# Small tiled matmuls of a hybrid decoder layer gathered into bursts, and weights converted one piece further ahead

## The chip, the cores and the metric

One core of one Trainium2 chip. Times are device microseconds of that core; the figure compared is the median of several executions.

## The reference, cut to what matters

One inference step of a decoder layer for 256 prompt tokens and 64 sample tokens (8 sequences of 8), 320 columns in all, in float32:

```
p = x @ w_in                          # 2048 -> 5408
y_lru  = rg_lru(conv(p[:1024])) * gelu(p[1024:2048])          # 8 blocks of 128 channels
y_rwkv = rwkv7_mix(p[2048:])          # 16 heads of 64; per token, per head:
#   S = S * w_t - (S kk_t) (kk_t a_t)^T + v_t k_t^T ;  o_t = S r_t ; group norm, bonus, gate
x = LN(ALPHA * x + concat(y_lru, y_rwkv) @ w_out)
x = LN(ALPHA * x + cross_attention(x, mem_k, mem_v, 4 heads of 512, 256 memory tokens) @ xa_wo)
x = LN(ALPHA * x + relu(x @ mlp_w1)**2 @ mlp_w2)              # 2048 -> 8192 -> 2048
```

The keys and values of the memory (`mem @ xa_wk`, `mem @ xa_wv`) and all final states are outputs too.

## The kernel before, in words

**Linear layers.** A weight comes in pieces of 128x1024 (512 KB), loaded by SyncE's queue into `wraw`. ScalarE rounds a piece to `wh` (the high part), and VectorE or GpSimd subtracts it to give `wl` (the low part); activations `u` are held in the same two parts. Each product of a 128x128 weight block is three TensorE matmuls: high x high, high x low, low x high (`mm_piece`, line 380). A piece holds 8 blocks, so 24 matmuls. The trace names the first two `ps<-u,wh` and the third `ps<-u,wl`. `Stream` (line 252) runs ahead: `get` (line 295) loads three pieces ahead and casts two ahead; there are 4 `wraw`, 3 `wh` and 3 `wl` buffers. `poll` issues the subtraction once the cast is done in planned time; which engine takes it is decided by `tt` (line 326), which adds `pool_wait` (6 us in the mixer, 0 after) to GpSimd's price.

**The stages.** In the mixer the input projection makes 43 tiles of 128 output columns: three code tiles, then r, k, v, x, g for each of eight pairs of heads. The memory's key projection follows (16 tiles of 256 columns), then the value projection, the output projection, the query projection with cross attention, its output projection, and the MLP.

**The planner.** Python generators emit the mixer's work, and `Sched` (line 117) decides at build time in which order the instructions stand in each engine's queue, by its own clock and costs. A generator yields `PE` ahead of TensorE work. `tick` (line 199) is called ahead of each group of three linear matmuls and emits every waiting TensorE step whose inputs are ready by the clock (plus 0.3 us), up to 2 us of them. So small matmuls stand between linear ones as soon as they are ready. `drain` (line 218) emits tasks in order of time with no linear work between.

**A pair of heads** (`rwkv`, line 624) takes these steps: two products for decay and rate (`code,lw`); head sums (128x32 tiling); scores of four chunks of 64 tokens (`AR,BK`, 64x64) and of the sample tokens; transposes (`K,BK`, `K,t`); a loop over four chunks; then centring, head sums, the gate product (`sg,lg`). Each chunk has three steps: a right-hand side (`S,AR` and `UV,GM`), a product with the inverse (`R,XT`), and the last step, which updates the state and the output (`UV,BT`, then `AR,S`, then `GM,UV`; names are moving operand, then stationary one). A product of 64x64 uses a quarter of the array, one of 128x64 half, and several stand beside each other; a float32 matmul appears as two records. `invert` (line 828) inverts a triangular matrix on GpSimd, with DMA round trips, and four TensorE steps (32x32); `sample` (line 906) does the 64 sample tokens in steps of its own.

**What holds pairs apart.** Pair p's transposes wait until pair p-2 is finished. When tile v of pair i is done, `on_win` (line 1023) drains pair i-3 if it still runs, and after the key projection everything is drained. `tmp` (line 519) has 18 work tiles. PSUM has 8 banks, one for each `ax()` (line 339).

Of the kernel before, what the change touches and what calls it, by code (L numbers as in the profile page):

```python
# [88 lines left out]
for _name, _w in (("mu", 27), ("w0", 8), ("a0", 8), ("kk", 8), ("ka", 8), ("rk", 8), ("lnw", 8), ("lnb", 8),  # L89
                  ("cw0", 8), ("cw1", 8), ("cw2", 8), ("cw3", 8), ("cb", 8), ("ba", 8), ("bx", 8), ("lam", 8),  # L90
                  ("g1", 16), ("b1", 16), ("g2", 16), ("b2", 16), ("g3", 16), ("b3", 16),
                  ("h0", 64), ("sh", 216), ("cv", 192)):
    VEC[_name] = _n
    _n += _w
NVEC = _n
# [10 lines left out]
NTMP = 18  # L106
NPB = 3
MARGIN = 0.3
QUEUE = 1.2
# [7 lines left out]
class Sched:  # L117
# [5 lines left out]
    def __init__(self):  # L123
        self.clock = 0.0
        self.free = {"V": 0.0, "A": 0.0, "G": 0.0}
        self.tasks = []
        self.cur = None
        self.table = 0
        self.poll = lambda: None

    def account(self, e, op, a, k):
# [4 lines left out]
        if e == "T":  # L136
            m = a[1].shape[-1]
            if a[1].dtype == F32R:
# [35 lines left out]
    def add(self, gen, name=None, after=0.0, eng=None):  # L174
        self.tasks.append(Task(gen, name, self.clock + after, eng is None, eng))
# [23 lines left out]
    def tick(self, budget=2.0):  # L199
        c0 = self.clock  # L200
        self.poll()
        moved = True
# [24 lines left out]
class Task:  # L227
    def __init__(self, gen, name, t, pe=True, eng=None):
        self.gen, self.name, self.t, self.pe, self.eng = gen, name, t, pe, eng


PE = "PE"
# [19 lines left out]
class Stream:  # L252


    def __init__(self, nc, sch, A, tt, raw, hp, lp, srcs, ahead_load, ahead_conv):
# [3 lines left out]
        self.al, self.ac = ahead_load, ahead_conv  # L259
        self.n_load = self.n_conv = 0  # L260
# [4 lines left out]
    def poll(self, upto=None):  # L265

        while self.pend:
# [6 lines left out]
            self.sch.cur = cur  # L274

# [19 lines left out]
    def get(self, i):  # L295
        while self.n_load < min(len(self.srcs), i + 1 + self.al):
# [7 lines left out]
def body(ctx, tc, I, O):  # L304
# [12 lines left out]
    pool_wait = [6.0]  # L317
# [19 lines left out]
    drp = ctx.enter_context(tc.tile_pool(name="dr", bufs=1, space=DRAM))  # L337

    def ax():
        return psp.tile([128, 512], F32, name="ps")  # L340
# [13 lines left out]

    sh_out = cst.tile([128, 27, 9], F32, name="sh_out")
# [1305 lines left out]
```

## Time and profile before

| what | value |
| --- | --- |
| median of three runs (lowest to highest) | 2049.2 us (2038.58 to 2050.24) |
| the profiled execution: its own time, its span | 2050.63 us, 2048.5 us |
| TensorE busy, matmul records | 1999.3 us (98%), 15750 |
| VectorE, ScalarE, GpSimd busy | 1054.7, 890.8, 430.3 us |
| mean granted clock of TensorE | 0.989 |
| weight pieces of the input projection, issue to landing | 4.7 us, 86 pieces |

TensorE's matmuls are pipelined and their ends are modelled, so that a record is longer than its share of the stream; what a matmul costs is read from the distance between starts. A busy TensorE can therefore still lose time between starts. The trace puts all engine work on one line, L246 (the wrapper `Eng` that accounts for it); instructions are told apart by their tiles.

### The profile page before, as it was taken

How to read it: one execution, taken by the hardware profiler on the slowest of the kernel's cores; microseconds unless marked ns; L12 is line 12 of the kernel's file. 1: busy time of each engine (PE TensorE's matmuls, PEld its weight loads, DVE VectorE, ACT ScalarE, POOL GpSimd, SP SyncE). 2: the span in 40 equal slices, each digit the busy share in tenths (PEclk: the TensorE clock that was granted, in tenths of full speed). 3: DMA queues.
4: the chain of work that ended last, by engine and by line, in shares of the span. 5: the costliest groups of instructions: out<-in, count | busy, mean ns of one | idle time of the engine just before them, and what ended most of it. 6: DMA issues, size and time to landing. Idle time of an engine off the chain costs nothing.

```text
span 2048.5 us, 38116 instructions
## 1 busy us (share of the span) xinstructions
PE 1999.3 (98%) x15750; PEld 1887.1 (92%) x15750; DVE 1054.7 (51%) x1604; ACT 890.8 (43%) x1452; POOL 430.3 (21%) x689
## 2 busy tenths in 40 slices
PE   8999999999999999999999999999999999999996
PEld 8987888788898998888899999999999999999996
DVE  6666666667545446544476444443444434443444
ACT  5655555455335335544334533334333333334333
POOL 0223022222214245322053300000000000001133
PEclk9999999999999999999999999999999999999998
DMA  7343343335467774688643444444444444445442
GB/s 249 127 125 99 102 132 119 106 109 172 140 197 249 241 213 150 239 318 305 234 142 120 144 147 152 151 148 151 148 154 145 154 148 152 150 149 152 147 147 90
DMA packets 120701, 333.79 MB, mean 163 GB/s; under 512 B 33056, under 2 KB 42304, under 8 KB 120528
## 3 DMA queue, kind: packets, MB, share of 16 engines
q1 hardware_dynamic: 105392, 279.59, 43.3%
q0 software_dynamic: 15136, 51.77, 7.0%
q8 instruction: 123, 2.02, 0.4%
q14 instruction: 50, 0.41, 0.1%
HBM read 315.66 MB, written 15.65 MB: 162 GB/s over the span
## 4 chain that ended last, share of the span: by engine, by line
PE 90%; DVE 3%; POOL 3%; issue 1%; DMA 1%; ACT 1%; SPq 0%; POOLq 0%; ACTq 0%; DVEq 0%
PE ps L246 90%; DVE wl L246 1%; DVE t L246 1%; POOL wl L246 1%; DVE u L246 1%; POOL tt L246 1%; POOL u L246 0%; POOL Xp L246 0%; ACT wh L246 0%; POOL r L246 0%; DMA t<-in_x 0%; DMA Xn<-bx 0%; DMA kv<-in_cache_k 0%; ACT u L246 0%; DMA Mp<-bm 0%
## 5 line engine op out<-in xcount | busy, mean ns | idle before, releaser
L246 DVE TENSOR_TENSOR wl<-wraw,wh 128x1024 fp32r<-128x1024 f32 x490 | 616.0, 1259 | 579.5 <-ACT wh L246 578.8
L246 ACT CAST wh<-wraw 128x1024 fp32r<-128x1024 f32 x502 | 526.1, 1048 | 652.9 <-PE ps L246 607.7
L246 PE MATMUL ps<-u,wh 128*128 128x320 f32 (+1 forms) x3424 | 764.0, 313 | 7.5 <-ACT u L246 6.6
L246 PE MATMUL ps<-r,wh 128*128 128x320 f32 x3072 | 681.9, 311 | 2.1 <-ACT r L246 1.8
L246 PEld LDWEIGHTS ps<-u,wh 128*128 128x128 f32 x3424 | 566.5, 190 | 27.9 <-issue 7.7
L246 PE MATMUL ps<-u,wl 128*128 128x320 f32 (+1 forms) x1712 | 525.9, 307 | 9.9 <-DVE wl L246 9.7
L246 PEld LDWEIGHTS ps<-r,wh 128*128 128x128 f32 x3072 | 515.8, 189 | 10.4 <-issue 7.5
L246 PE MATMUL ps<-r,wl 128*128 128x320 f32 x1536 | 476.5, 310 | 4.7 <-POOL wl L246 2.5
L246 PEld LDWEIGHTS ps<-u,wl 128*128 128x128 f32 x1712 | 324.8, 190 | 12.4 <-DVE wl L246 12.4
L246 PEld LDWEIGHTS ps<-r,wl 128*128 128x128 f32 x1536 | 289.8, 189 | 5.2 <-POOL wl L246 2.8
L246 PE MATMUL ps<-h,wh 128*128 128x320 f32 x1024 | 225.6, 309 | 0.0
L246 POOL TENSOR_TENSOR r<-r 128x320 f32<-128x320 f32 x64 | 46.0, 720 | 724.6 <-ACT r L246 724.6
L246 PEld LDWEIGHTS ps<-h,wh 128*128 128x128 f32 x1024 | 171.4, 188 | 0.2
L246 PE MATMUL ps<-h,wl 128*128 128x320 f32 x512 | 158.2, 309 | 0.0
L246 DVE TENSOR_TENSOR u<-u,ps 128x320 f32<-128x320 f32 x134 | 61.7, 484 | 78.2 <-PE ps L246 75.5
L246 ACT ACTIVATE r<-ps 128x320 f32<-128x320 f32 x64 | 28.0, 437 | 157.8 <-PE ps L246 157.8
L246 PEld LDWEIGHTS ps<-h,wl 128*128 128x128 f32 x512 | 96.1, 188 | 0.0
L246 POOL TENSOR_TENSOR tt<-Mp,Xp 40x15 f32<-40x15 f32 (+7 forms) x120 | 46.8, 390 | 191.8 <-DMA Mp<-bm 183.5
L246 POOL TENSOR_TENSOR s<-s,u 128x320 f32<-128x320 f32 x42 | 65.3, 1554 | 92.5 <-DVE u L246 92.3
L246 PE MATMUL ps<-wh,u 128*128 128x512 f32 x256 | 79.9, 391 | 0.0
L246 ACT ACT_TABLE_LOAD x48 | 61.6, 1283 | 9.2 <-DVE mxs L246 7.7
L246 PEld LDWEIGHTS ps<-wh,u 128*128 128x128 f32 x256 | 48.1, 188 | 10.1
(239 smaller groups left out, 1574.6 us busy)
## 6 DMA issues: line engine op xcount, KB each, us to landing
wraw<-in_w SPq DMA_DIRECT2D x256, 512.0 KB, 3.5
wraw<-in_w_in SPq DMA_DIRECT2D x86, 512.0 KB, 4.7
wraw<-in_wk SPq DMA_DIRECT2D x32, 512.0 KB, 4.7
wraw<-in_wv SPq DMA_DIRECT2D x32, 512.0 KB, 4.8
wraw<-in_w_out SPq DMA_DIRECT2D x32, 512.0 KB, 4.1
kv<-in_cache_k POOLq DMA_DIRECT2D x32, 512.0 KB, 6.6
wraw<-in_wq SPq DMA_DIRECT2D x32, 512.0 KB, 5.1
kv<-in_cache_v POOLq DMA_DIRECT2D x32, 512.0 KB, 8.7
```

Source lines behind the costliest of these rows:

```text
L246: r = f(*a, **k)
```

## The change

`Sched` knows the tiling of each TensorE step (`Mode`, rows x columns, with the number of PSUM banks it needs) and adds 0.093 us to its clock where the tiling changes. `tick` emits 128x128 steps at once, others only if 2.2 us have passed since the last of them or at least four are ready; then it prefers the tiling that the array has. Steps that need more banks than are free by the planner's count wait (`room`: 8, and 7 from tile 37 on).

In `rwkv` the scores of chunks and sample become one step of four banks, and the two groups of transposes one of three; the state product of the output (`AR,S`) moves from the last step of a chunk to the step of `R,XT`; the product `bv` moves ahead. In `sample` the identity product joins the right-hand side, and the last two steps become one, with its masked operand always made by VectorE. The decay products and head sums now wait for a burst. `attend_sample` yields the 128x32 tiling for its products.

`Stream` casts three pieces ahead, with 3 `wraw`, 4 `wh` and 4 `wl` buffers; it issues a load when the subtraction three pieces before is issued. `pool_wait` is 50 us in the mixer and 2 us after it. Work tiles fall from 18 of 356 columns to 16 of 348; the shift state is loaded into one of them, and three output tiles live only in the mixer.

```diff
-NTMP = 18
+NTMP = 16
 NPB = 3
 MARGIN = 0.3
+TURN = 0.093
+GAP = 2.2
+FULL = (128, 128)
...
+            mode = tuple(32 if x <= 32 else 64 if x <= 64 else 128 for x in (a[1].shape[0], m))
+            if mode != self.mode:
+                self.clock += TURN
+                self.mode = mode
...
-            task.pe = x == PE
+            task.pe = isinstance(x, Mode)
+            if task.pe:
+                task.mode, task.need = x.mode, x.need
...
-    def tick(self, budget=2.0):
-        c0 = self.clock
+    def tick(self):
         self.poll()
+        self.others()
+        ready, c0 = self.ready(), self.clock
+        tiled = c0 >= self.burst + GAP or sum(t.mode != FULL for t in ready) >= 4
+        while self.clock - c0 <= 3.0:
+            ready = [t for t in ready if tiled or t.mode == FULL]
+            if not ready:
+                break
+            self.step(next((t for t in ready if t.mode == self.mode), ready[0]))
+            if self.mode != FULL:
+                self.burst = self.clock
+            self.others()
+            ready = self.ready()
...
+    def ready(self):
+        return [t for t in self.tasks if t.pe and t.t + MARGIN <= self.clock and self.fits(t)]
+    def fits(self, task):
+        return not task.pe or self.room is None or self.live + task.need <= self.room
...
             for task in list(self.tasks):
-                if task not in self.tasks:
+                if task not in self.tasks or task.pe:
                     continue
-                if task.pe:
-                    ok = task.t + MARGIN <= self.clock and self.clock - c0 <= budget
-                else:
-                    ok = task.t <= self.clock + 0.1
-                    if task.eng:
-                        ok = ok and self.free[task.eng] <= self.clock + QUEUE
-                if ok:
+                if task.t <= self.clock + 0.1 and (not task.eng or self.free[task.eng] <= self.clock + QUEUE):
                     self.step(task)
                     moved = True
...
-            t = min(self.tasks, key=lambda t: t.t)
+            t = min([t for t in self.tasks if self.fits(t)], key=lambda t: t.t)
...
+PE, PE_HH, PE_FH, PE_FQ, PE_QQ, PE_HF = (Mode(*x) for x in ((128, 128), (64, 64), (128, 64), (128, 32), (32, 32), (64, 128)))
...
             cur, self.sch.cur = self.sch.cur, None
             self.tt(l, t, h.bitcast(F32), ALU.subtract)
             self.sch.cur = cur
+            self.n_low += 1
+            if self.n_load < len(self.srcs) and self.n_load < self.n_low + 3:
+                self.load()
...
     def get(self, i):
-        while self.n_load < min(len(self.srcs), i + 1 + self.al):
+        while self.n_load < min(len(self.srcs), self.n_low + 3):
             self.load()
         while self.n_conv < min(self.n_load, i + 1 + min(i, self.ac)):
...
-    pool_wait = [6.0]
+    pool_wait = [50.0]
...
-    rawp = ctx.enter_context(tc.tile_pool(name="wraw", bufs=4))
-    hp = ctx.enter_context(tc.tile_pool(name="wh", bufs=3))
-    lp = ctx.enter_context(tc.tile_pool(name="wl", bufs=3))
+    rawp = ctx.enter_context(tc.tile_pool(name="wraw", bufs=3))
+    hp = ctx.enter_context(tc.tile_pool(name="wh", bufs=4))
+    lp = ctx.enter_context(tc.tile_pool(name="wl", bufs=4))
...
+            yield PE_HF(2)
             pw, pa = ax(), ax()
             T.matmul(pw[:, :NTOK], lw[0:64, :], code[0:64, :], start=True, stop=True)
...
+            yield PE_HH(4)
             pg = [ax(), ax()]
             for c in range(4):
                 for s in range(2):
                     for i, h in enumerate(HS):
                         o, a = slots(i)[s]
                         mm(pg[i][o, c * 128:c * 128 + 128], BK[h, c, a, :], AR[h, c, :, :])
-            yield
-            for i in range(2):
-                V.tensor_mul(GM[:, i, 0:4], pg[i].rearrange("p (c a t) -> p c a t", c=4, a=2),
-                             MU[:, 0:1].to_broadcast([128, 4, 2, 64]))
-            sch.cur.t -= 1.0
-            yield PE
-            B4 = pp.tile([128, 2, 64], F32, name="B4")
-            UV4 = pp.tile([128, 2, 64], F32, name="UV4")
...
-            pt = [ax(), ax()]
+            yield PE_HH(3)
+            pt, pv = [ax(), ax()], ax()
             for c in range(4):
                 for s in range(2):
                     for i, h in enumerate(HS):
                         o, a = slots(i)[s]
                         mm(pt[i][o, c * 64:c * 64 + 64], BK[h, c, a, :], ident[h, h])
-            yield
-            for i in range(2):
-                copy(BT[:, :, 64 * i:64 * i + 64], pt[i][:, :256].rearrange("p (c x) -> p c x", c=4))
-            yield PE
-            pv = ax()
             for c in range(4):
                 for h in HS:
                     mm(pv[h, c * 64:c * 64 + 64], zv[h, c * 64:c * 64 + 64], ident[h, h])
             yield
+            for i in range(2):
+                copy(BT[:, :, 64 * i:64 * i + 64], pt[i][:, :256].rearrange("p (c x) -> p c x", c=4))
             for i, h in enumerate(HS):
...
+                yield PE_HH
                 for o in HS:
                     mm(pr[o, 64:128], XT[o, c, :], R[o, :])
+                if c:
+                    for h in HS:
+                        mm(po[h, c * 64:c * 64 + 64], S[h, :], AR[h, c, 1, :], True, False)
                 for i, o in enumerate(HS[::-1]):
                     copy(UV[o, c, i, :], pr[o, 64:128])
-                yield PE
+                yield PE_FH
                 for i, h in enumerate(HS):
                     mm(pr[h, 128:192], BT[:, c, 64 * i:64 * i + 64], UV[:, c, i, :])
                 Sn = p2.tile([128, 64], F32, name="S")
                     V.scalar_tensor_tensor(Sn, pr[:, 128:192], PT[:, c:c + 1], ts_, op0=mult, op1=add)
                 else:
                     V.tensor_scalar(Sn, pr[:, 128:192], PT[:, 0:1], None, op0=mult)
-                if c:
-                    for h in HS:
-                        mm(po[h, c * 64:c * 64 + 64], S[h, :], AR[h, c, 1, :], True, False)
+                free()
                 for i, h in enumerate(HS):
                     mm(po[h, c * 64:c * 64 + 64], UV[:, c, i, :], GM[:, i, c, 1, :], not c, True)
                 S = Sn
-                yield PE
+                if c < 3:
+                    yield PE_HH
+            yield
             nc.gpsimd.dma_start(O["Sp"][p], S)
...
-            yield PE
-            pr = ax()
+            free()
+            yield PE_HH(2)
+            pr, po = ax(), ax()
             for i, h in enumerate(HS):
                 mm(pr[HS[1 - i], 0:64], RO[h, 0, :], ident[h, h], True, False)
             for i, h in enumerate(HS):
                 mm(pr[HS[1 - i], 0:64], GM[h, i, 4, 0, :], UV[h, i, :], False, True)
             R = p1.tile([128, 64], F32, name="R4")
             copy(R, pr[:, 0:64])
-            yield PE
+            for h in HS:
+                mm(po[h, 0:64], ident[h, h], RO[h, 1, :], True, False)
+            yield PE_HH
             for o in HS:
                 mm(pr[o, 64:128], XT[o, 4, :], R[o, :])
             for i, o in enumerate(HS[::-1]):
                 copy(UV[o, i], pr[o, 64:128])
+            free()
             yield
             um = [p1.tile([128, 8, 64], F32, name=f"um{i}") for i in range(2)]
             for i in range(2):
-                tt(um[i], UV[:, i:i + 1, :].to_broadcast([128, 8, 64]),
-                                BM.unsqueeze(2).to_broadcast([128, 8, 64]), mult)
-            sch.cur.t -= 2.0
-            yield PE
-            po = ax()
+                V.tensor_tensor(um[i], UV[:, i:i + 1, :].to_broadcast([128, 8, 64]),
+                                BM.unsqueeze(2).to_broadcast([128, 8, 64]), op=mult)
+            yield PE_FH
             for i, h in enumerate(HS):
-                mm(po[h, 0:64], UV[:, i, :], GM[:, i, 4, 1, :], True, False)
-            for h in HS:
-                mm(po[h, 0:64], ident[h, h], RO[h, 1, :], False, True)
+                mm(po[h, 0:64], UV[:, i, :], GM[:, i, 4, 1, :], False, True)
             res["po"] = po
-            yield 1.5
-            yield PE
             pu = ax()
             for i, h in enumerate(HS):
                 mm(pu[h, :], B4[:, i, :], um[i].rearrange("p b i -> p (b i)"))
             yield
             V.tensor_add(S0, S0, pu.rearrange("p (b i) -> p b i", b=8))
+            free()
...
                 sch.drain("der")
+                sch.room = 8
+            elif m == 37:
+                sch.room = 7
...
-        pool_wait[0] = 0.0
+        sch.room = None
+        pool_wait[0] = 2.0
...
+            yield PE_FQ
             ps = ax()
```

## Rows read from the trace of the kernel before

**Rows 1.** Busy time by stretch: span of stretch, engines (x instructions), granted clock, DMA.
```profile
50.00:613.70 563.70, 548.72 (x5856) 479.70 (x5855) 353.20 (x695) 296.86 (x589) 135.62 (x349) 0.98 0.42 130
1200.00:2000.00 800.00, 799.86 (x5452) 799.44 (x5451) 340.11 (x367) 280.39 (x347) 65.59 (x75) 1.00 0.48 150
162.30:165.70 3.40, 2.99 (x12) 2.66 (x12) 0.35 (x1) 0.00 (x0) 0.90 (x4) 0.50 0.53 178
527.50:537.70 10.20, 9.83 (x125) 8.64 (x126) 6.21 (x14) 3.13 (x4) 0.00 (x0) 0.50 0.61 220
```

**Rows 2.** Groups by form, TensorE, 0 to 613.7 us: busy, mean ns, idle before.
```profile
L246 PE MATMUL ps<-u,wl 128*128 128x320 f32 x688 | 214.9, 312 | 7.2 <-DVE wl L246 7.0
...
L246 PE MATMUL ps<-u,wl 128*128 128x256 f32 x256 | 73.6, 288 | 1.8 <-DVE wl L246 1.8
```

**Rows 3.** Timeline of TensorE, 221.8 to 226.1 us: start, length, instruction.
```profile
221.78 0.31 PE L246 MATMUL ps<-u,wl 128*128 128x320 f32 x1
222.02 0.33 PE L246 MATMUL ps<-R,XT 64*64 64x64 f32 x4
...
222.68 0.31 PE L246 MATMUL ps<-u,wl 128*128 128x320 f32 x1
...
224.63 0.31 PE L246 MATMUL ps<-u,wl 128*128 128x320 f32 x1
224.87 0.34 PE L246 MATMUL ps<-UV,BT 128*64 128x64 f32 x4
225.14 0.33 PE L246 MATMUL ps<-AR,S 64*64 64x64 f32 x4
225.40 0.34 PE L246 MATMUL ps<-GM,UV 128*64 128x64 f32 x4
...
226.07 0.31 PE L246 MATMUL ps<-u,wl 128*128 128x320 f32 x1
```

**Rows 4.** Timeline of TensorE, two steps of one tiling.
```profile
322.57 0.31 PE L246 MATMUL ps<-u,wl 128*128 128x320 f32 x1
322.81 0.33 PE L246 MATMUL ps<-S,AR 64*64 64x64 f32 x4
322.97 0.28 PE L246 MATMUL ps<-UV,GM 64*64 64x64 f32 x4
...
323.58 0.31 PE L246 MATMUL ps<-u,wl 128*128 128x320 f32 x1
```

**Rows 5.** Timeline of TensorE: first and last small products, end of the mixer.
```profile
54.72 0.81 PE L246 MATMUL ps<-code,lw 64*128 64x320 f32 x4
...
584.37 1.28 PE L246 MATMUL ps<-sg,lg 128*128 128x320 f32 x4
...
613.20 0.40 PE L246 MATMUL ps<-u,wh 128*128 128x256 f32 x2
...
613.56 0.40 PE L246 MATMUL ps<-wh,u 128*128 128x512 f32 x1
```

**Rows 6.** Timeline of all engines around the longest wait for a low part.
```profile
159.20 2.38 POOL L246 TENSOR_TENSOR wl<-wraw,wh 128x1024 fp32r<-128x1024 f32 x1 [3.21 <-ACT wh L246]
159.26 3.39 DVE L246 TENSOR_TENSOR wl<-wraw,wh 128x1024 fp32r<-128x1024 f32 x1
...
162.71 0.63 PE L246 MATMUL ps<-u,wl 128*128 128x320 f32 x1 [2.51 <-DVE wl L246]
```

**Rows 7.** Timeline of TensorE, two more waits for low parts.
```profile
361.70 0.42 PE L246 MATMUL ps<-u,wl 128*128 128x320 f32 x1 [2.29 <-DVE wl L246]
...
1135.56 0.63 PE L246 MATMUL ps<-r,wl 128*128 128x320 f32 x1 [2.52 <-POOL wl L246]
```

**Rows 8.** Timeline of TensorE where the linear stream stops for a drain.
```profile
444.37 0.33 PE L246 MATMUL ps<-S,AR 64*64 64x64 f32 x4
...
445.22 0.33 PE L246 MATMUL ps<-R,XT 64*64 64x64 f32 x4 [0.41 <-ACT R L246]
...
450.68 0.56 PE L246 MATMUL ps<-u,wh 128*128 128x320 f32 x2
```

More of the change, by code (lines that the diff above doesn't have):

```diff
@@ L128, in __init__ @@
         self.table = 0
+        self.mode, self.burst = FULL, 0.0
+        self.live, self.room = 0, None
         self.poll = lambda: None
@@ L174, in add @@
     def add(self, gen, name=None, after=0.0, eng=None):
-        self.tasks.append(Task(gen, name, self.clock + after, eng is None, eng))
+        self.tasks.append(Task(gen, name, self.clock + after, eng))
     def run(self, gen, name=None):
@@ L227, with __init__, __call__ @@
 class Task:
-    def __init__(self, gen, name, t, pe=True, eng=None):
-        self.gen, self.name, self.t, self.pe, self.eng = gen, name, t, pe, eng
-PE = "PE"
+    def __init__(self, gen, name, t, eng=None):
+        self.gen, self.name, self.t, self.pe, self.eng = gen, name, t, False, eng
+        self.mode, self.need = None, 0
+class Mode:
+    def __init__(self, rows, cols, need=1):
+        self.mode, self.need = (rows, cols), need
+    def __call__(self, need):
+        return Mode(*self.mode, need)
+PE, PE_HH, PE_FH, PE_FQ, PE_QQ, PE_HF = (Mode(*x) for x in ((128, 128), (64, 64), (128, 64), (128, 32), (32, 32), (64, 128)))
 class Eng:
@@ L353, in der @@
         return E[:, DER[name] + i:DER[name] + i + w]
-    sh_out = cst.tile([128, 27, 9], F32, name="sh_out")
-    cv_out = cst.tile([128, 8, 9, 3], F32, name="cv_out")
-    h_out = cst.tile([128, 8, 9], F32, name="h_out")
     srcs = []
@@ L501, in body @@
         p1 = mx_ctx.enter_context(tc.tile_pool(name="one", bufs=1))
+        sh_out = p1.tile([128, 27, 9], F32, name="sh_out")
+        cv_out = p1.tile([128, 8, 9, 3], F32, name="cv_out")
+        h_out = p1.tile([128, 8, 9], F32, name="h_out")
         KM = p1.tile([128, C_N - C_BO], F32, name="KM")
@@ L515, in derive0 @@
             V.tensor_scalar(omu, mu, -1.0, 1.0, op0=mult, op1=add)
-            V.tensor_tensor(shm, vec("sh", 0, 216).rearrange("p (j b) -> p j b", b=8),
+            V.tensor_tensor(shm, xr["sh"].rearrange("p (j b) -> p j b", b=8),
                             mu.unsqueeze(2).to_broadcast([128, 27, 8]), op=mult)
         def tmp(n=NTOK):
-            return tp.tile([128, 356], F32, name="t")[:, :n]
-        xr = {}
+            return tp.tile([128, 348], F32, name="t")[:, :n]
+        xr = {"n": 0}
         def x_tile(kt):
             xr[kt] = t = tmp()
+            xr["n"] += 1
             nc.sync.dma_start(t, I["x"][kt // 2][:, kt % 2, :])
-            if kt % 2 and st.n_load < 4:
+            if kt % 2 and st.n_load < 3:
                 st.load()
             if kt == 7:
-                nc.sync.dma_start(W, I["vecs"])
+                nc.sync.dma_start(W, I["vecs"][:, 0:NVEC])
+                xr["sh"] = tmp(216)
+                nc.sync.dma_start(xr["sh"], I["vecs"][:, NVEC:NVEC + 216])
                 nc.sync.dma_start(K, I["cst"][:, 0:C_BO])
@@ L534, in x_prod @@
         def x_prod(kt):
-            while len(xr) < min(kt + 4, KT):
-                x_tile(len(xr))
+            while xr["n"] < min(kt + 4, KT):
+                x_tile(xr["n"])
             X.put(kt, xr[kt])
@@ L668, in rwkv @@
             V.scalar_tensor_tensor(kk, zk, der("kkh", p), pq, op0=mult, op1=mult)
+            bv = pp.tile([128, NTOK], F32, name="bv")
+            V.tensor_mul(bv, zv, pb[:, :NTOK])
+            free(2)
             V.scalar_tensor_tensor(X2[:, 1], ta, 1.0, kk, op0=add, op1=mult)
@@ L687, in slots @@
                 return (HS[i], 0), (HS[1 - i], 1)
-            yield PE
+            B4 = pp.tile([128, 2, 64], F32, name="B4")
+            UV4 = pp.tile([128, 2, 64], F32, name="UV4")
+            yield PE_HH(4)
             pg = [ax(), ax()]
@@ L722, in rwkv @@
                 copy(UV4[h, i], p4[i][h, 192:256])
-            bv = pp.tile([128, NTOK], F32, name="bv")
-            V.tensor_mul(bv, zv, pb[:, :NTOK])
+            free(4)
             PT = pp.tile([128, 12], F32, name="PT")
@@ L748, in rwkv @@
             yield
+            for i in range(2):
+                copy(BT[:, :, 64 * i:64 * i + 64], pt[i][:, :256].rearrange("p (c x) -> p c x", c=4))
             for i, h in enumerate(HS):
                 copy(UV[h, :, i, :], pv[h, :256].rearrange("p (c i) -> p c i", c=4))
+            free(3)
             bk_used.add(p)
@@ L973, in lru_task @@
                                    cx[:, 259:347].rearrange("p (b t) -> p b t", t=11)[:, :, 0:8], op0=mult, op1=add)
-            A.copy(cv_out[:, i, :, :], ue[:, 256:355].rearrange("p (b t) -> p b t", t=11)[:, :, 0:3])
-            yield PE
+            A.copy(cv_out[:, i, :, :], bass.AP(tensor=ue.tensor, offset=ue.offset + 256, ap=[ue.ap[0], [11, 9], [1, 3]]))
+            yield PE(2)
             pa, px = ax(), ax()
@@ L1403, in attend_sample @@
                 release(h, 0, 4 * g2, 4 * g2 + 3)
[L1404 removed]
+                if g2 == 0:
+                    yield PE_FQ
+            yield
             while sch.alive(("atts", h - 1)):
```

63 lines of the change are left out of this document (40 added, 23 removed).

## The prediction

> **What bounds the kernel now.** I read the windows first. From 1200 to 2000 us, in the MLP, TensorE issues 5452 matmuls in 800 us, 0.1467 us each, and is busy throughout: nothing there can shrink. From 50 to 613.7 us, in the mixer, it is also nearly always busy, but the work is mixed; VectorE is busy 353 of 564 us [rows 1]. Next the groups by form in the mixer: 688 low-part products of 320 columns and 256 of 256 columns, each with two high-part products, so 2064 and 768 linear matmuls [rows 2]. At 0.1467 and 0.120 us (three of the latter fill the 0.36 us from 613.20 to 613.56 [rows 5]) they need 302.8 + 92.2 = 395 us. The mixer ends at 613.6 us, where the V projection begins [rows 5]. So about 219 us go elsewhere: the RWKV and LRU matmuls, changes between tilings, waits for weights, and the start.
>
> **The price of leaving the linear stream.** The timeline gives it. Two low-part products stand 3 x 0.147 = 0.44 us apart when only linear work is between them. With the four records of one 64x64 step between them they stand 222.68 - 221.78 = 0.90 us apart: the excursion cost 0.46 us [rows 3]. With two such steps of the same tiling it is 323.58 - 322.57 - 0.44 = 0.57 us [rows 4]. So the second step costs 0.11 us, and **0.35 us of every excursion is entry and exit**. The chunk step of three tilings in a row costs 226.07 - 224.63 - 0.44 = 1.00 us [rows 3]: 0.35 + 3 x 0.11, and 0.16 us for each of the two changes inside. Along the timeline I count 165 excursions with a tiling other than 128x128, the first at 54.72 us and all before the last small product at 584.37 [rows 5], with 99 changes inside them: 165 x 0.35 + 99 x 0.16 = 74 us is the pool that the change can draw on.
>
> **The change part by part, against the profiled execution's 2050.6 us** (span 2048.5 and 2.1 around it; 1.4 above the median of the runs).
>
> 1. The state product of a chunk (64x64) moves from between two 128x64 products into the step before it. Both changes inside go: 2 x 0.16 x 24 chunks (three of each of eight pairs) = **7.7 us** less. It now stands ahead of the copies of UV by 0.11 us, within what a step waits anyway.
> 2. Three pairs of steps become one each (the two score products, the two groups of transposes, the last two products of the sample task): 24 excursions at 0.35 = 8.4 us. The sample task's identity product also moves to a step of its own tiling: 8 x 0.16 = 1.3 us. Together **9.7 us**; where two were already joined by chance (rarely: I find both alone in most pairs), less.
> 3. The gathering: tiled steps wait until 2.2 us of planned time have passed since the last one, or four are ready. Of the 164 spaces between excursions, 120 are under 2.2 us, and joining every such excursion to the burst that it follows leaves 92. The steps now arrive later too, so chains spread out again; each chain can make only one step in a burst. I take 105 left of the 141 that remain after 2 (ends: 92 and 130). A joined step saves 0.35 us in the same tiling and 0.19 in another, 0.27 on average: 36 x 0.27 = **9.7 us** (3 to 13). Steps 1 to 3 give 27 us, between 18 and 32.
> 4. Weights. In the mixer PE waits 7.2 + 1.8 = 9.0 us for low parts [rows 2]. The longest case shows one cause: GpSimd and VectorE subtract at the same time, VectorE's takes 3.39 us and PE waits 2.51 [rows 6]; the other 2.29 us wait is VectorE late by its own queue [rows 7]. A fourth pair of buffers converts one piece earlier: 24 matmuls, 3.5 us, longer than either wait. GpSimd does none in the mixer any more; it did two, so VectorE gains two subtractions. After the first stall the granted clock is 0.50 for 3.4 us, in which 12 matmuls run that need 1.76 at full clock [rows 1]: with 0.4 of stall inside, 1.2 us lost, and I count two such cases. Together 11.4; **9 us** taken, since VectorE's queue stays in order. Ends 0 and 11.4.
> 5. After the mixer GpSimd is taken only when VectorE is 2 us late. At 1135.56 us PE waited 2.52 us for GpSimd's low part [rows 7], and by the price above a slow-clock stretch follows: **3 us** taken, ends 0 and 3.7. Tilings change too rarely there to matter; the sample attention's bursts I cost at nothing, its chains being covered by the query projection.
> 6. What is added. Raw buffers fall from four to three and a load waits for a subtraction; SyncE's queue behind it holds the inversion's transfers, the low-rank weights and the states. A load is still issued two to three pieces (7 to 10 us) before its cast, and its landing is covered by that. Of two fewer work tiles I see no row: nothing taken; ends 0 and the 2.3 us of one late copy chain [rows 7] per pair, 18 us. The bank limit delays the four-bank step when two chunk loops overlap; they rarely do. The real cost is the waiting itself: a pair has about 25 tiled steps, some 20 in sequence, and each waits up to 2.2 us. Ends: nothing (always ready later than the gap) and 1.1 (ready at random in it). I take 0.5, as a step must wait for a copy and two queues before it is ready at all; that makes a pair 10 us longer. Pair p must be finished when the third v tile after it is done, or it is drained with no linear work beside it. That happens already: from 444.37 to 450.68 us the stream stops for pair 4, and in it a step waits 0.41 us for a copy [rows 8]; most of these 6.3 us are work that would come later anyway. More such drains, at five v tiles and the end, with two or three such waits each, so 1 us idle: **6 us** added, ends 0 and 35 (the second rival's price, cut to what still leaves a gain).
>
> The sum: 27 + 9 + 3 - 6 = 33 us less, 2017.6 against the profile, **2016** as a median.
>
> **Rivals.**
> *The waits eat the gain* (2029 to 2049, no change by my bound). For it: the last pair finishes at 584.4 with its final gate product, and the mixer's linear work ends at 613.6 [rows 5], 29 us of slack, which shrinks by about 10 as that stretch gets shorter and by 10 as the chain gets longer. If bursts stay single (130 left, 18 us from steps 1 to 3), half of step 4 comes, and drains cost 12: 18 + 5 + 1 - 12 = 12 us less, 2037. Against it: 1 and 2 do not depend on the gathering, and give 17 us by themselves.
>
> *Slower: pairs outlast their three periods.* Place: the v tiles of pairs 3 to 7 and the end of the mixer, six drains. If each of 25 steps waits 1.1 us, a pair is 27 us longer, while three periods are 15 shorter: some 40 us of a chain are then run without cover at each drain. A drained step idles PE by 0.4 us [rows 8] to 2.5 us [rows 6]. The gain of 39 us is gone at 6.5 us of idle per drain and the 1% bound is crossed at 10: 2050.6 - 39 + 6 x 11 = 2078. Against it: the drain in the rows shows a 0.41 us wait as its longest, since all other chains advance in it too.
>
> *VectorE becomes the bound.* A burst hands VectorE and ScalarE the copies of several steps at once, so its second step is ready later, and the next burst comes later. VectorE is at 63% in the mixer, and its 353 us over a mixer shorter by 36 are 67% [rows 1]. If the second copy of 100 bursts costs PE half of the row's 0.41 us [rows 8], that is 20 us: 2050.6 - 39 + 20 = 2032. The Trainium skill (TensorEngine Tiling (Array Packing), section PSUM Bottleneck) says that tiling speeds up the products but not the evacuation of PSUM, so that the copies may become the limit. By that rule the gathering would give back most of what it saves; the trace bears it out only weakly, in that one short wait [rows 8].
>
> *More than forecast:* 92 excursions, all of 4 and 5, no added drain, and the 10.2 us stretch at half clock at 527.5 us [rows 1], gone: at half clock the same work takes nearly twice as long, so 4.6 us. 32 + 11 + 4 + 5 = 52 less, 1998.
>
> *The change doesn't do what it says:* the gap never binds, because in the planner's own time steps lie further apart than in the trace. Then only 1, 2, 4 and 5 act: 17 + 9 + 3 - 0 = 29 us, 2022, hardly another result.
>
> **How the numbers follow.** Forecast as worked, with its near misses (2003 to 2028): 0.50. More than forecast: 0.14. The gap never binds: 0.06, with the forecast's sign. Waits eat the gain or VectorE binds: 0.20, within 1%. Slower: 0.10. One per cent, 20.5 us, is about what a measurement of this kernel can tell from no change: its three runs lie 11.7 us apart. Faster by over 1% means under 2028.7: 0.50 + 0.14 + 0.06 less 0.02 of near misses, 0.68; within 1% 0.22; slower 0.10. The range leaves out the slower rival and the best of the best case: 1993 to 2045.
>
> **What would show it.** Step 1: the chunk's last step holds 128x64 products alone. Steps 2 and 3: excursions counted as here, near 105, each with two or more tilings; 140 refutes 3. Step 4: no subtraction on GpSimd before the V projection, and idle time ahead of low-part products in the mixer under 3 us. Step 6: linear stops longer than 8 us at v tiles; final gate product of the last pair after the last key-projection matmul. The V projection should begin near 580 us (613.6 - 36 + 6 = 584); a start after 605 us makes the forecast wrong whatever the reason.

## The result: 0.6% slower, and the profile after

The kernel after takes 2056.57 us (median of 9 runs), the kernel before 2044.37 (9 runs): a ratio of 1.0063 [1.0046, 1.0079]. The forecast was 2016, the upper end of its range 2045. The profiled execution after took 2060.96 us (span 2059.2), 10.3 more than the one before.

Where it went, by stage: the V projection begins at 629.08 us instead of 613.56 [rows 5], 15.5 later. From there to the end of the span it is 1430.1 us instead of 1434.9, 4.8 less. The loss is in the mixer alone. Windows of the kernel after, columns as in [rows 1]; the third is one of its half-clock stretches:

```profile
50.00:629.10 579.10, 541.85 (x5882) 488.08 (x5881) 352.66 (x694) 298.82 (x598) 128.85 (x347) 0.95 0.42 127
1200.00:2000.00 800.00, 799.86 (x5452) 799.44 (x5451) 340.13 (x367) 281.50 (x351) 64.05 (x75) 1.00 0.47 150
540.60:550.80 10.20, 9.67 (x91) 9.18 (x92) 4.62 (x10) 6.35 (x13) 1.07 (x2) 0.50 0.74 241
```

The MLP is what it was. In the mixer TensorE is idle for 37.3 us of the first window (579.1 less 541.85), before for 15.0 [rows 1], and the granted clock is 0.95 instead of 0.98. What it waits for stands in the waits of TensorE, 20 to 630 us (total us, times, longest):

```profile
PE ps L284 <- DMA Xn<-bx: 12.3, 4, 5.6
PE ps L284 <- DVE UV L284: 8.5, 3, 4.9
PE ps L284 <- DVE S L284: 5.8, 2, 4.7
PE ps L284 <- ACT u L284: 4.6, 3, 2.4
PE ps L284 <- DVE R L284: 3.4, 1, 3.4
PE ps L284 <- DVE um L284: 3.0, 1, 3.0
```

The same view of the kernel before, 20 to 613.7 us:

```profile
PE ps L246 <- DVE wl L246: 8.8, 7, 2.5
PE ps L246 <- DMA Xn<-bx: 2.0, 1, 2.0
PE ps L246 <- DVE UV L246: 1.8, 3, 0.7
```

The waits for low parts (`wl`) are gone. `Xn`, the inverse that comes back from DRAM, took their place, with copies on VectorE and casts on ScalarE. All waits together were 14.9 us, 6.1 without the low parts; after they are 39.7. The groups of after that answer to [rows 2] show the same: no idle time ahead of any low-part product.

```profile
L284 PE MATMUL ps<-u,wl 128*128 128x320 f32 x688 | 217.9, 317 | 0.0
...
L284 PE MATMUL ps<-u,wl 128*128 128x256 f32 x256 | 74.4, 291 | 0.0
```

**One inversion, followed.** It starts when VectorE has masked the scores (`GM`); `GM` goes to DRAM, comes back as `Mp`, GpSimd does 30 small operations, and the result goes out (`bx`) and back in (`Xn`). The rows of a pair in the kernel after, from the timeline of all engines (start, length, instruction, idle time before it and what ended it):

```profile
320.50 1.67 DVE L284 TENSOR_TENSOR GM<-ps,KM 128x512 f32<-128x512 f32 x4
...
324.13 1.42 SPq L320 DMA_DIRECT2D wraw<-in_w_in  x2
...
325.60 1.26 SPq L892 DMA_DIRECT2D bm<-GM  x2
...
333.01 0.56 POOL L284 TENSOR_TENSOR tt<-Mp,Xp 40x15 f32<-40x15 f32 x1 [22.74 <-DMA Mp<-bm]
...
346.90 0.21 POOL L284 TENSOR_TENSOR Xp<-Xp,tt 40x15 f32<-40x15 f32 x1
347.14 0.31 SPq L912 DMA_DIRECT2D bx<-Xp  x1
...
349.13 1.26 SPq L917 DMA_DIRECT2D Xn<-bx  x2
...
352.37 0.51 DVE L284 STREAM_TRANSPOSE XT<-Xn 128x320 f32<-128x320 f32 x1 [5.96 <-DMA Xn<-bx]
352.41 0.52 PE L284 MATMUL ps<-Xn,GM 16*32 16x16 f32 x40 [2.87 <-DMA Xn<-bx]
```

Read three things. GpSimd's part takes 14.1 us (333.01 to 347.11). The last group of `GM` ends at 322.17, but its transfer is issued at 325.60, behind two weight loads in SyncE's queue. And VectorE had stood 5.96 us, TensorE 2.87, when `Xn` landed. The same pair in the kernel before (the rows end with the transpose, ahead of which VectorE had not stood idle):

```profile
313.20 0.48 DVE L246 TENSOR_TENSOR GM<-ps,KM 128x128 f32<-128x128 f32 x2
...
313.51 2.09 SPq L835 DMA_DIRECT2D bm<-GM  x2
...
336.74 1.26 SPq L860 DMA_DIRECT2D Xn<-bx  x2
...
344.18 0.51 DVE L246 STREAM_TRANSPOSE XT<-Xn 128x320 f32<-128x320 f32 x1
```

Over the eight pairs the transpose of `Xn` begins a mean of 29.3 us after the last `GM` before and 29.5 after. That is not the length of the chain: before, VectorE came to the transpose after `Xn` had landed in seven pairs of eight; after, it stood waiting in seven. The chain is read from the issue of the `Xn` transfer, a mean of 22.9 us after the last `GM` before and 26.0 after: it got 3.1 us longer. `bm` goes out at once in all eight pairs before; in five pairs after it goes out 2.3 to 3.4 us late. Meanwhile TensorE's product of `Xn` moved 2.4 us closer: it begins 32.8 us after `GM` before, having waited in one pair of eight, and 30.4 after, having waited in four. So the consumers lost some 5.5 us of cover, over half of it to a longer chain. ("Cover" is the time between a chain's end and the moment at which its result is wanted.)

What waits for the inversion on VectorE holds up what stands behind it in VectorE's queue, as the rows at 283.72 below show. Waits of VectorE, kernel after, 50 to 630 us:

```profile
DVE t L284 <- POOL t L284: 31.2, 7, 6.5
DVE XT L284 <- DMA Xn<-bx: 26.2, 7, 6.0
```

The same two before, 50 to 613.7 us:

```profile
DVE t L246 <- POOL t L246: 4.3, 3, 2.4
DVE XT L246 <- DMA Xn<-bx: 3.2, 1, 3.2
```

The first of the two after is a memset for the LRU's scan on GpSimd, in six of the seven cases among or behind an inversion's 30 operations. What that does to TensorE:

```profile
283.72 0.82 DVE L284 TENSOR_TENSOR_SCAN t<-t 128x320 f32<-128x320 f32 x1 [6.47 <-POOL t L284]
...
285.05 0.22 DVE L284 COPY UV<-ps 64x64 f32<-64x64 f32 x1
...
285.32 0.48 PE L284 MATMUL ps<-UV,BT 128*64 128x64 f32 x4 [4.86 <-DVE UV L284]
```

The copy of `UV` has nothing to do with the scan; it stands behind it.

### The profile page after: what moved, and what is told of

Its sections match the earlier page's. It is cut to its first block, busy times and chain, and to the rows that moved or that the text cites. A ratio compares the mean times of both kernels' runs of the same rounds, so it can differ in the third digit from the quotient of the medians.

```text
span 2059.2 us, 38107 instructions
## 1 busy us (share of the span) xinstructions
PE 1986.5 (96%) x15750; PEld 1889.1 (92%) x15750; DVE 1049.3 (51%) x1608; ACT 890.4 (43%) x1459; POOL 407.6 (20%) x677
## 4 chain that ended last, share of the span: by engine, by line
PE 85%; POOL 5%; DMA 4%; DVE 3%; issue 1%; ACT 1%; SPq 0%; POOLq 0%; ACTq 0%; DVEq 0%
PE ps L284 85%; POOL Xp L284 2%; POOL tt L284 2%; DMA Mp<-bm 1%; DMA bm<-GM 1%; DVE wl L284 1%; DMA t<-in_x 1%; DMA Xn<-bx 0%; DVE t L284 0%; DMA wraw<-in_w_in 0%; POOL u L284 0%; DMA t<-in_mem 0%; ACT u L284 0%; DVE GM L284 0%; DVE u L284 0%
## 5 line engine op out<-in xcount | busy, mean ns | idle before, releaser
L284 PEld LDWEIGHTS ps<-u,wh 128*128 128x128 f32 x3424 | 577.1, 193 | 32.0 <-ACT u L284 12.2
L284 PEld LDWEIGHTS ps<-u,wl 128*128 128x128 f32 x1712 | 329.6, 193 | 0.0
L284 PEld LDWEIGHTS ps<-wh,u 128*128 128x128 f32 x256 | 48.1, 188 | 10.1
```

Source lines behind the costliest of these rows:

```text
L284: r = f(*a, **k)
```

## The experiments

The theory: the planner sets consumers by prices under which an inversion is too short, and the saved TensorE time uncovered that. It prices GpSimd's 30 operations at 0.15 us each plus 2.1 ns for each element of a row, 7.4 us where the trace has 14.1, and each transfer at 2.5 us. Rivals: the copy behind the memset; the new weight stream (fewer raw buffers, loads that wait in SyncE's queue); the gathering itself. Each ratio is to the kernel before, run alongside; its 95% interval stands beside it. Medians of different experiments were taken against different runs of the kernel before, so a difference of a few us between them is read from the ratios. The edits are shown condensed, old on the left, new on the right.

**Memsets of the scan and of `P` from GpSimd to VectorE; honest prices; both.**

```diff
-G.memset(P[:, 0:1], 1.0)                  +V.memset(P[:, 0:1], 1.0)         # e1, e3 (also a0)
-c = 0.15 + 2.1e-3 * n   # GpSimd          +c = 0.36 + 2.1e-3 * n            # e2, e3, mixer only
-def dma(self, t=2.5):                     +def dma(self, t=3.1):            # e2, e3
```

> The changed kernel, with two small memsets of the work tiles (the first column of the decay products' scan, the eight reset columns of the LRU scan) moved from GpSimd to VectorE. Theory of lost slack: GpSimd's queue holds these memsets behind an inversion of 14 us, VectorE waits 31 us for them in the mixer and hands the wait on to TensorE; without it TensorE's waits for VectorE (UV, S, R, um, 20.7 us) fall by half or more and with them two or three stretches at half clock: 10 to 22 us less, 2035 to 2047. Rival, SyncE's queue held up by weight loads that wait for a free raw buffer: these memsets are not the cause, 0 to 4 us less.

> The changed kernel, with the planner's price of a GpSimd instruction in the mixer raised from 0.15 to 0.36 us plus its elements, and a transfer from 2.5 to 3.1 us: the order of work changes, not the work. Theory of lost slack: consumers of an inversion are placed about 8 us later, the waits for its transfer (12.3 us on TensorE, 26 us on VectorE) mostly go, and half-clock stretches with them: 18 to 35 us less, 2022 to 2039, although pairs last longer. Rival, SyncE's queue: the transfers still start 2 to 3 us late behind weight loads, a third of the gain at most, 2046 to 2054. Rival, pairs too long: later consumers mean more drains at the v tiles, no gain or a loss, 2055 to 2070.

> The two edits before together. Theory of lost slack: all but some 10 us of the new waits are gone and the kernel keeps the 24 us of tilings and 9 us of weights: 2008 to 2028, clearly faster than the kernel before. Rivals: not below 2040.

The memsets alone: 2073.34 us, 1.0137 [1.0115, 1.016], a miss. VectorE's wait for the memset went away, and its wait for `Xn` rose from 26.2 to 51.5 us: next in its queue stood the transpose. TensorE waits 18.0 us for `UV` instead of 8.5. The honest prices: 2039.28, 0.9971 [0.9959, 0.9983], 17 us less than after, and TensorE's wait for `Xn` falls from 12.3 to 2.3 us. Both: 2027.17, 0.9908 [0.9884, 0.9932]. So moving the memsets costs 17 us at the old prices and gains 12 us at the honest ones: at the old prices VectorE only meets the next wait sooner. The waits of the first two, VectorE's for `Xn` of the memset kernel, then TensorE's of the honest one:

```profile
DVE XT L284 <- DMA Xn<-bx: 51.5, 7, 10.0
```

```profile
PE ps L285 <- DMA Xn<-bx: 2.3, 1, 2.3
```

**The planner's charge for a change of tiling, by itself.** Before with such a charge (e4); after without it (e13).

```diff
+if mode != self.mode: self.clock += 0.175; self.mode = mode     # e4, in the kernel before
-TURN = 0.093                               +TURN = 0.0          # e13, in the kernel after
```

> The kernel before, with one thing added: its planner's clock counts 0.175 us for every change of tiling, which is what the trace shows a change to cost. No instruction is added or removed. Theory of lost slack: the kernel before was covered because its planner did not know of some 75 us that TensorE spends on changes; an honest clock for TensorE alone lets consumers be placed earlier among the linear matmuls, and waits for the inversion and for VectorE appear: 10 to 35 us slower, 2054 to 2079. Rival: a better clock makes a better order, 0 to 15 us faster.

> The changed kernel with TURN 0: the planner's clock no longer counts changes of tiling, as before the change; the gathering, the chunk steps and the weights stay. Theory of lost slack: TensorE's real time runs ahead of the planner's by some 40 us more, consumers of an inversion stand later, its waits (12.3 us on TensorE, 26 on VectorE) fall by half or more: 2036 to 2050. Rival: the order is only noisier, 2052 to 2062.

In the kernel before, the charge raises TensorE's wait for `Xn` from 2.0 to 15.1 us (five waits), but the time is 2047.78, 1.0018 [1.0002, 1.0035]: the mechanism is seen, its size was missed, and the waits for low parts fell from 8.8 to 1.1 at the same time. In the kernel after, without the charge, it is 2055.0, 1.0053 [1.0036, 1.007], and `Xn` still costs 9.6 us. In the kernel before the charge does bring the consumer closer: TensorE's product of `Xn` begins a mean of 27.7 us after the last `GM` instead of 32.8. In the kernel after, taking it off moves that product only from 30.4 to 31.2 us. So the charge can take cover away, but it isn't what took most of it in the change: that part of the theory falls.

```profile
PE ps L252 <- DMA Xn<-bx: 15.1, 5, 4.5
...
PE ps L252 <- DVE wl L252: 1.1, 1, 1.1
```

**The gathering off, on top of both edits; both edits in the kernel before.**

```diff
-GAP = 2.2                                  +GAP = 0.0           # e5, else as e3
```

> The kernel of e3 (both edits, 2027 us) with GAP 0 in place of 2.2: tiled steps are emitted as soon as they are ready, everything else as in e3. Theory: gathering is worth its price once the inversion's consumers are placed right; 20 to 40 more excursions at 0.3 us come back: 2033 to 2043. Rival: the waiting costs the chains as much as it saves: 2020 to 2030.

> The kernel before with the two edits of e3 (GpSimd priced at 0.36 us and its elements in the mixer, transfers at 3.1 us, two memsets on VectorE). Theory of lost slack: it needs them little, since it waits only once, 2.0 us, for an inversion, with one stretch of 10 us at half clock after it: 2036 to 2045. Rival: honest prices are worth as much to any version, and the change is worth nothing: 2015 to 2030.

Without the gap: 2037.33, 0.9950 [0.9932, 0.9968]. The gap is worth 0.4% (0.9950 against 0.9908; 10.2 us between the medians), and excursions are 151 without it, 111 with it. Not all of that is tilings: the mixer of e5 also has 4.1 us more of waits (24.4 against 20.3) and 10.2 us more at half clock. The kernel before with both edits: 2044.28, 0.9981 [0.9966, 0.9995]. At these prices the change is worth 0.7% (0.9908 against 0.9981).

**The weight part, apart.** Old stream (4 raw, 3 high, 3 low buffers, casts two ahead) in e3 and in after; the new one alone in before.

```diff
-rawp/hp/lp bufs = 3/4/4; casts 3 ahead     +4/3/3; 2 ahead      # e6 on e3, e9 on after
-rawp/hp/lp bufs = 4/3/3; casts 2 ahead     +3/4/4; 3 ahead      # e7 on before, pool_wait 50, 16 tmps
```

> The kernel of e3 with the old weight stream: four raw buffers, three high and three low ones, loads three pieces ahead, casts two ahead; GpSimd's share as in e3. Theory: the third piece of lead is what took away the waits for low parts; some 5 to 9 us of them come back with a stretch or two at half clock: 2032 to 2042. Rival, SyncE's queue held by loads that wait for a raw buffer: ScalarE's waits for weights and memory tiles (16.6 and 17.5 us in e3) go, transfers of the inversion start 2 to 3 us earlier: 2012 to 2024.

> The kernel before with only the weight part of the change: three pieces ahead, three raw and four high and low buffers, GpSimd's waiting price 50 and 2 us, 16 narrower work tiles. Prediction's step 4 and 5: 9 + 3 us less, 2030 to 2037. Theory of lost slack: the waits for low parts (9 us) covered chains too, so half of it comes back as waits for the inversion: 2036 to 2044. Rival, SyncE's queue: loads that wait for a raw buffer delay other transfers, no gain or a loss, 2044 to 2055.

> The changed kernel with the old weight stream (four raw buffers, three high and low ones, loads three and casts two pieces ahead), nothing else undone. Theory of lost slack: the inversion's waits stay, since they come from the planner's prices, and waits for low parts return: 2052 to 2066. Rival, SyncE's queue: e6 showed that the old stream takes away every wait for a load; if those waits are the main loss of the change, this is 2032 to 2046.

All three are draws, against what was expected of e6 and e7. On e3, 2027.15 against 2027.17: the waits for low parts come back, 15.1 us of them, others go. In the kernel before the new stream gives 2047.53, 1.0004 [0.9992, 1.0016]: low parts no longer wait, but TensorE waits 10.1 us for casts of the memory's tiles, and ScalarE 19.7 us for those tiles' loads (0.9 before). On after, 2054.96, 1.0046 [1.0032, 1.0059], which can't be told from after.

```profile
PE ps L246 <- ACT u L246: 10.1, 3, 7.8
```

```profile
ACT u L246 <- DMA t<-in_mem: 19.7, 5, 7.3
```

**SyncE's queue.** A weight load is issued as soon as it is planned, and waits at the head of the queue until the subtraction has freed its raw buffer. That wait of SyncE's queue is 227.5 us before and 360.6 after, over 50 to the V projection:

```profile
SPq L279 <- DVE wl L246: 227.5, 54, 12.5
```

```profile
SPq L320 <- DVE wl L284: 360.6, 87, 16.7
```

Whatever stands behind comes late: a memory tile's load was issued at 466.07 us, right after such a weight load. ScalarE waited 6.73 us for the tile, VectorE 4.83 us for ScalarE's cast of it, and TensorE 4.66 us for a sum (`S`) that stands behind in VectorE's queue:

```profile
465.68 0.34 SPq L320 DMA_DIRECT2D wraw<-in_wk  x1
466.07 1.85 SPq L1121 DMA_DIRECT2D t<-in_mem  x4
...
470.84 1.44 ACT L284 CAST u<-t 128x256 fp32r<-128x256 f32 x4 [6.73 <-DMA t<-in_mem]
471.27 1.46 DVE L284 TENSOR_TENSOR u<-t,u 128x256 fp32r<-128x256 f32 x4 [4.83 <-ACT u L284]
...
472.79 0.68 DVE L284 TENSOR_TENSOR S<-S,ps 128x512 f32<-128x512 f32 x1
...
473.52 1.43 PE L284 MATMUL ps<-code,lw 64*128 64x320 f32 x2 [4.66 <-DVE S L284]
```

The edits: issue the load only when the planner's clock says that the subtraction is done; load memory tiles one ahead.

```diff
-self.load()                                +self.due.append(self.sch.free["V"])
+while self.due and self.due[0] <= self.sch.clock: self.due.pop(0); self.load()    # e10, e11, e14
+for k in (kt, kt + 1): mem_tile(k)         # e12, e14: the next memory tile's load too
```

> The changed kernel; a weight load stands in SyncE's queue only once the subtraction that frees its raw buffer is done by the planner's clock, instead of directly behind it, so the queue is held for less time and the transfers behind it start earlier. SyncE's queue theory: transfers of the inversion start at once (2 to 3 us earlier in five pairs), memory tiles too: 2038 to 2050. Theory of lost slack alone: the inversion is still priced 9 us too short, 2050 to 2058.

> The kernel of e3 with the later load issue of e10. If SyncE's queue causes ScalarE's waits for loads in e3 (16.6 us for weights, 17.5 for memory tiles) half of them go: 2016 to 2025. If those waits come from the transfers themselves, no change: 2024 to 2031.

> The kernel of e3 with the tiles of the memory input loaded one tile earlier than they are rounded. ScalarE's waits for memory tiles (17.5 us) mostly go and with them TensorE's waits behind ScalarE (8.1 and 2.3 us): 2014 to 2024. If the queue as such is late, the wait moves to the weights: 2024 to 2030.

> e11 and e12 together (dearer GpSimd and transfers in the planner, two memsets on VectorE, weight loads issued later, memory tiles loaded one ahead). If the two act on different waits: 2014 to 2022. If both only shift the same queue: 2020 to 2028.

Late loads alone take after to 2044.68, 0.9988 [0.9975, 1.0001]: 12 us, so the queue is a cause by itself. Its wait at weight loads falls only in part, from 360.6 to 321.9 us (longest 10.2 instead of 16.7); the issue of the `Xn` transfer moves from 26.0 to 23.9 us behind the last `GM` (22.7 with the old stream, e9), VectorE's wait for the memset falls from 31.2 to 19.1 us, TensorE's for `Xn` from 12.3 to 7.9. On top of e3 they add nothing (2026.32, 0.9903 [0.9881, 0.9924]): with honest prices the late transfers are covered too. Lookahead for the memory tiles on e3 gives 2022.89, 0.9884 [0.9864, 0.9903]; both 2022.02, 0.9893 [0.9869, 0.9917]. All these intervals overlap that of e3, so no gain of lookahead is shown.

**Dearer still.** On e14, GpSimd 0.5 us and transfers 4.0 (e15), 0.65 and 5.0 (e17); the prices of e15, memsets and lookahead in the kernel before (e16); after's planner with them and the old stream (e18).

```diff
-self.pool_c = 0.36; dma(t=3.1)             +0.5; 4.0    # e15, e16, e18    +0.65; 5.0    # e17
```

> e14 with the planner's price of a GpSimd instruction at 0.5 us plus elements and a transfer at 4.0 us, above what the trace shows. If what is left of the waits still comes from prices that are too low, 2010 to 2018. If pairs become too long for their three periods, drains at the v tiles grow: 2024 to 2040.

> The kernel before with the prices of e15 (GpSimd 0.5 us plus elements, a transfer 4.0 us), the two memsets on VectorE and memory tiles loaded one ahead; the tilings, the chunk steps and the weights are as before. Theory: the kernel before has margin, so dear prices are worth little to it and the gain of e15 is the change's own: 2034 to 2048. Rival: the prices alone do it: 2010 to 2026.

> e15 with GpSimd at 0.65 us plus elements and a transfer at 5.0 us. If e15 still waits for prices, 2006 to 2012. If its margin is enough already, pairs only last longer and drains grow: 2013 to 2025.

> The changed kernel's planner, gathering and chunk steps with the prices of e15, the two memsets on VectorE, memory tiles one ahead, and the old weight stream of four raw buffers and two casts ahead. If the new stream's waits for loads are what is left in e15 (10 us of PE waits), and dear prices keep low parts in time as in e16 (3 us): the tilings' 24 us come on top of e16, 2001 to 2011. If low parts are late again as in e6 (15 us): 2012 to 2026.

The best is e15: 2013.52, **0.9854 [0.9836, 0.9871]**, faster than both kernels. In its mixer TensorE waits 12.3 us in all, 6.8 us are at half clock, excursions are 117 as in the kernel after, and the V projection begins at 583 us, where the forecast had put it (584); that is luck, since e15 holds edits that the forecast knew nothing of. Its window and its waits for `Xn`:

```profile
50.00:583.00 533.00, 522.53 (x5879) 470.62 (x5878) 351.00 (x700) 304.06 (x609) 135.56 (x332) 0.99 0.45 138
```

```profile
PE ps L285 <- DMA Xn<-bx: 0.3, 1, 0.3
```

Dearer again is worse: 2033.56, 0.9943 [0.9923, 0.9962], with 34 us at half clock. And such prices help the kernel before too: e16 is 2027.46, 0.9904 [0.9884, 0.9924], where little gain was expected (2034 to 2048). With the old stream e18 is 2021.11, 0.9874 [0.9848, 0.99], 8.3 us of waits for low parts are back, and the hope of more was not met; its interval overlaps that of e15, so a gain of the new stream is not shown at these prices either. Set beside e16, the change (with the later loads that its stream needs) holds 0.5% of e15's gain (0.9854 against 0.9904, some 10 us), the prices, memsets and lookahead 1%. And e16 waits only 3.5 us in its mixer and has no half clock there: part of what the tilings save in e15 still goes into waits.

## Why the prediction was wrong, step by step

**The step that failed is step 6**, "**6 us** added, ends 0 and 35": TensorE's other waits in the mixer rose by 34 us (6.1 to 39.7), and the half clock that follows them took some 16 more. Together 50 us stand where the step had 6, and 35 as its upper end. Two of its arguments failed: that what is added would be idle time in drains, and that the new weight stream costs nothing because a load's landing is covered.

- **Steps 1 and 2, right.** The chunk's last step is `UV,BT` and `GM,UV` alone (at 349.09 and 349.26 us), both 128x64. Changes inside excursions fell from 99 to 59.
- **Step 3, right in its count.** Excursions fell from 165 to 117, where 105 were forecast and 140 would have refuted it. By the forecast's prices, 117 x 0.35 + 59 x 0.16 = 50 us against 74: steps 1 to 3 gave 24 us, 27 were forecast. A second estimate agrees: take from each mixer its waits and 0.44 us for each us at half clock (worked out below), and 591 us are left before and 565 after, 26 less; by the same account e15 and e18 are 20 us below e16. For the gathering alone it leaves 5 us (e5 570, e3 565), about half of step 3's 9.7; each figure is from one profile.
- **Step 4, right in what it removes, wrong in what it is worth.** The 9.0 us are 0.0, no subtraction of the mixer is on GpSimd. But alone it gives nothing (e7): waits for memory tiles that stand behind weight loads took it back, and step 6 had priced those loads at nothing.
- **Step 5, right in size, not in its cause.** 4.8 us, 3 taken, and the wait at 1135.56 us is gone. But GpSimd still makes 8 low parts behind the mixer (10 before), and with the old stream and GpSimd's new price (e9) the wait is there again. So the new stream, with its piece more of lead, took it away, not the price:

```profile
1136.96 0.41 PE L284 MATMUL ps<-r,wl 128*128 128x320 f32 x1 [2.53 <-POOL wl L284]
```

- **Step 6, where it was looked for.** The prediction looked at drains, where linear work runs out. There was no such loss at the end: the last pair's gate product is at 611.40 us, 17.7 ahead of the V projection (29 before [rows 5]). And linear work stops for over 4 us at two drains before (from 203.77 and 444.13) and at the same two after (211.81 and 465.86). The last of these did reach the sign of 8 us that the prediction had set (9.0 us), but its one long wait, 4.66 us, is that for the late memory tile above. The other six such stops of after, 4.0 to 6.8 us, have linear work waiting behind them: in each TensorE stands for 2.1 to 5.6 us at a small product whose operand is late.
- **Of the queue and its buffers** the prediction said that a load's landing is covered. Not always: ScalarE's waits for the input projection's pieces rose from 2.1 to 11.1 us (rows below), though TensorE waited for none of those casts. And what stands behind such a load was not costed. The prediction named the inversion's transfers as queued there, then priced only the load; the late transfers made the chain 3.1 us longer.

```profile
ACT wh L246 <- DMA wraw<-in_w_in: 2.1, 3, 1.0
```

```profile
ACT wh L284 <- DMA wraw<-in_w_in: 11.1, 4, 5.2
```

- **Half clock.** Three stretches of the mixer at granted clock 0.50 (1.2 GHz, the lower of two levels), 17.1 us in all, became nine, 54.6 us. At 0.50, three matmuls of 256 columns take 0.64 us (rows below) instead of 0.36 [rows 5]: an estimated 0.44 us lost of each us, 16 us for the 37 more.

```profile
541.13 0.48 PE L284 MATMUL ps<-R,XT 64*64 64x64 f32 x4 [3.43 <-DVE R L284]
...
542.55 0.63 PE L284 MATMUL ps<-u,wh 128*128 128x256 f32 x2
...
543.19 0.63 PE L284 MATMUL ps<-u,wh 128*128 128x256 f32 x2
```

The balance against the profile of before: -24 - 9 - 5 + 34 + 16 = +12, where the profiles show +10.3. In it 24 and 16 are estimates.

**The rivals.** "The waits eat the gain" came nearest, but by waits in mid-stream, not by slack at the end. "Slower" had its place wrong, the drains: one long wait of 4.66 us is in them. "VectorE becomes the bound" did not happen: it is busy 352.7 us as before, 61% of a longer window. Its queue's order made the waits, not its load, so the rule on the evacuation of PSUM that was weighed there (the Trainium skill, TensorEngine Tiling (Array Packing), PSUM Bottleneck) isn't what these traces show.

**What stays open.** Why the consumers came 2.4 us closer: by e13 the charge for tilings alone makes 0.8 of it; that a stretch of planned time now holds less real time, since excursions got cheaper, fits but was only argued. Why dear prices gave the kernel before 1% (e16), though it hardly waited for an inversion: in e16 low parts wait 3.0 us instead of 8.8 and no stretch is at half clock, but which of e16's edits did that was not tried. e1's 17 us over after are shared out among waits that moved, not settled one by one. The limit on PSUM banks was not undone in any run, and the 16 work tiles were tried apart from the gathering only together with the new stream (e7). The two causes, prices and queue, overlap: 29 us by e3, 12 by e10, and nothing by the second on top of the first.

## What to carry to other kernels

Where a planner writes in-order queues, the price of a slow side chain must be right before the main stream is made shorter: the time that the stream loses was the chain's cover (e2 and e3 fit this, and more prices than one were changed in them). Where a consumer begins does not tell how long its chain is, unless the consumer waited. Judge a wait by what stands behind it in the same queue, a DMA-issuing queue included, and expect a wait that is taken away to reappear at the next instruction of that queue (e1). Set a chain's planned lead by experiment, since too much costs as well (e15 against e17).

## What the runs showed of the hardware

- GpSimd's operations of 40x15 to 40x64 stand 0.30 to 0.38 us apart when undisturbed (333.95 to 334.25 for 40x28), and some take up to 1.2 us; 30 of them took 14.1 us, 0.47 each.
- Each of the nine stretches at granted clock 0.50 in the mixer of after begins inside a wait of TensorE of 2.0 to 5.6 us, or within 1.0 us of its end, such as the 10.2 us from 540.60, which begin inside the wait of 3.43 us that ends at 541.13. That added nearly half to the price of the new waits (an estimated 16 us to 34).
- An inversion's four transfers to DRAM and back (`bm`, `Mp`, `bx`, `Xn`) took, in the pair of the rows, 5.0, 2.4, 2.0 and 3.2 us from issue to the next step, 12.6 in all, where the planner of the change has 2.5 for each.
